# A fused two-block layer on one core: state outputs with the tables as moving operands, their regrouping on TensorE, and four smaller edits

## The chip, the core and the metric

The kernel runs on one core of a Trainium2 chip. The metric is the device time of one execution in microseconds (us); the median of three runs of the kernel before is 1020.39 us (1019.31 to 1023.4).

## The reference

Two blocks run one after the other on 512 tokens of width 1024, in fp32. The first is a norm, a gated causal convolution beside an attention over dilated windows, a projection of both (each normed first) that is added to x, and a gated feed-forward layer. The second block is the hybrid layer of which this change touches most:

```python
h = rms_norm_2(x, norm_g) * (1 + scale[:, None]) + shift[:, None]
xa, za, q, k, v, zb, qi, ki, wi, ga, gb = jnp.split(h @ w_in, IN_SPLITS, axis=-1)
ya = jax.nn.gelu(s5_mixer(xa, a_re, a_im, b_re, b_im, c_re, c_im, d_skip, log_dt))
g = ya @ w_glu + b_glu
ya = (g[..., :512] * jax.nn.sigmoid(g[..., 512:]) * jax.nn.silu(za)) @ w_a_o
yb = (dsa_mixer(q, k, v, qi, ki, wi) * jax.nn.silu(zb)) @ w_b_o
merged = jax.nn.sigmoid(ga) * ya + jax.nn.sigmoid(gb) * yb
x = x + gate[:, None] * (merged @ w_out)
return rms_norm_2(x, final_g)
```

`s5_mixer` is a state space model: 32 groups of 16 channels, each with 64 complex states, h_t = a h_(t-1) + B u_t and y_t = Re(C h_t) + D u_t. `dsa_mixer` is an attention that keeps the 128 best keys of each query.

## The kernel before

Activations lie as [features x 512 tokens]. A projection splits weights and activations into a high and a low part and issues three matmuls per 128 rows of the contraction (`mm3`, lines 193 to 195); in this text such a group is a triple. Weights stream through SP's queue in units of 512 KB, three units ahead, and are split by ACT (line 97) and DVE (line 98).

The order of TensorE's work is written as generators. The attention of a block asks for so many steps of a `filler` per head (`fill`), and each `yield` of a filler is a step; a tile scheduler then places the instructions of the other engines, with a priority lead (`high_priority`) for some.

*First block.* `mix_out` makes eight outputs of 128 rows, each of four triples (k = 0 to 3) over the normed branch, `ch`/`cl` for the convolution. The branch's root of the mean square (`rms`, then `rsqrt`: twelve DVE steps) is started at the first output; `spread` (line 236) turns it into a row on PE at the third. While the feed-forward layer runs, `ssm_tables` makes the tables of the state space model in four chunks, one `yield` at a time: `ca`, the table of the states' decays and C; `bts` (line 934); and `tt`, a block triangle of direct terms. They are stored to memory (`tabs`).

*Second block.* `gates` is the filler of the last attention: four projections for `szb`, four for `sza`, six of the eight for `thb` (tanh), then for each of the four chunks `chunk_out`, and after chunks 0 and 1 one more of the `thb`. `chunk_out(c)` copies the states into `hs` with GpSimd (POOL), loads `cat` and `tt` (two buffers under one tag, so the next chunk's loads wait for this chunk's matmuls), and issues for each of eight groups a matmul of `cat` with `hs` (line 1208) and one of `tt` with the inputs `U` (line 1209): table as the stationary operand of 128 x 128, 64 columns moving. Then comes gelu (ACT, DVE), eight stores `yad` and one load `yl` that bring the result from [step and channel x group and block] to [group and channel x time], and the split into `sh` and `sl` for the GLU projection.

The attention between those steps is scores (lines 254, 255), `z` (DVE, line 258), exp (ACT, line 262), transposes of the probabilities into two `tp` buffers of PSUM (line 306), their copies `pT` (ACT, line 312) and products with the values (line 283).

*Tail.* The final norm runs over two token halves: squares, a sum by PE (lines 1383, 1386), `rms_of` (DVE), `spread`, products and stores.

Of the kernel before, what the change touches and what calls it, by code (L numbers as in the profile page):

```python
# [9 lines left out]
F = mybir.dt.float32  # L10
R = mybir.dt.float32r
I32 = mybir.dt.int32
AF = mybir.ActivationFunctionType
OP = mybir.AluOpType
# [4 lines left out]
S = 512  # L19
D = 1024  # L20
P = 128
EPS = 1e-6
# [3 lines left out]
LEAD = 800  # L26
NT1 = 13
KS = 3
RAW = 3
WARM = 8  # L30
FILLA = (3.0, 4.0, 5.0, 2.6)
# [3 lines left out]
class K:  # L35
# [185 lines left out]

    def rms_of(self, pool, p, n, tag, room=None):
        toks = p.shape[1] // P
        d = pool.tile([P, 4, P], F, name="spd")[:, :toks]
        self.V.tensor_mul(d, p.rearrange("p (i t) -> p i t", t=P),
                          self.ident[:, None, :].to_broadcast([P, toks, P]))
        s = pool.tile([P, 4], F, name=tag + "s")[:, :toks]
        self.V.tensor_reduce(s, d, axis=AX.X, op=OP.add)
        return self.rsqrt(pool, s, 1.0 / n, EPS, tag, room)

# [85 lines left out]
    def mixer(self):  # L316
# [179 lines left out]
        def conv():  # L496
# [43 lines left out]
            for _ in range(3):  # L540
                yield
            yield from mix_out(ch, sqc)

        def mix_out(ys, sq):

            pend = []
            for n in range(8):
                if n % 2 == 0:
                    wh, wl = self.w()
                p = self.acc()  # L550
                cs = slice(n % 2 * P, n % 2 * P + P)
                yield from self.steps(p, (wh[:, :, cs], wl[:, :, cs]), ys)
                with self.tc.high_priority(offset=LEAD):
                    if n == 0:
                        r = self.rms(sm, [sq], 512, "rx")
                    if n == 2:
                        Rn = self.spread(sm, r, sm.tile([P, S], F, name="Rx"))
                pend.append((n, p))
                if n >= 2:
                    for m, p in pend:  # L560
                        t = at.tile([P, S], F, name="z", bufs=2)
                        V.tensor_mul(t, p, Rn)
                        V.tensor_add(x1[m], x1[m], t)
                    pend = []
                if n == 2:
                    for _ in range(4):
                        yield
# [10 lines left out]
        self.drain()  # L578
        self.run(mix_out(yh, sqa))
        cst.close()  # L580
# [4 lines left out]
    def ffn(self, x1):  # L585
# [10 lines left out]
        tabs = ExitStack()  # L596
        table = self.ssm_tables(tabs)
        for _ in range(2):
# [221 lines left out]

    def ssm_tables(self, st):
        nc, a, V, A, G, T = self.nc, self.a, self.V, self.A, self.G, self.T
# [51 lines left out]
        yield  # L874
        nr = p.tile([P, 48], F, name="snr")
        V.tensor_scalar(nr, pr[:, 1], -1.0, None, op0=OP.add)
# [27 lines left out]
        yield  # L904
        self.tabs = self.dram.tile([3, 4, P, S * 2], F, name="tabs")
        for c in range(4):
            gs = slice(8 * c, 8 * c + 8)
            def table(x, y, nj, name):
# [17 lines left out]
                                ca[:, :, 1:].rearrange("p g j x -> p g (j x)"))  # L926
            bts = p.tile([P, 8, P], F, name="bts", tag="io")
            kk = p.tile([16, 8, P], F, name="kk")
# [20 lines left out]
            V.tensor_add(kk[:, :, 0:16], kk[:, :, 0:16], de)  # L949
            tt = p.tile([P, 8, P], F, name="tt", tag="io")  # L950
            G.memset(tt, 0.0)
            for j in range(8):
                s = 7 - j
                nc.sync.dma_start(tt[16 * j:16 * j + 16, :, 16 * s:], kk[:, :, 0:P - 16 * s])
            nc.sync.dma_start(self.tabs[1, c], tt.rearrange("p g x -> p (g x)"))

# [57 lines left out]
    def hybrid(self, xs, second, close, out):  # L1014
# [174 lines left out]

        yad = self.dram.tile([4, P, S], F, name="yad")  # L1190
        y4 = yad.rearrange("j (g p) (s c) -> j s p g c", p=16, c=64)
        sv = []

        def chunk_out(sso, c):
# [10 lines left out]
            py = self.acc()  # L1205
            for g in range(8):
                o = py[:, g * 64:(g + 1) * 64]
                T.matmul(o, ca[:, g], hs[:, g], start=True, stop=False)  # L1208
                T.matmul(o, tt[:, g], U[:, 8 * c + g], start=False, stop=True)  # L1209
                yield  # L1210
            ys = sso.tile([P, S], F, name="ys")
# [5 lines left out]
            A.activation(y2, y2, AF.Tanh, scale=0.7978845608028654)  # L1217
            V.scalar_tensor_tensor(ys, y2, 1.0, ys, op0=OP.add, op1=OP.mult)
            for s in range(8):
                nc.sync.dma_start(y4[c, s], ys[16 * s:16 * s + 16].rearrange("p (g c) -> p g c", c=64))  # L1220
            yl = sso.tile([P, 8, 64], F, name="yl")
            nc.sync.dma_start(yl.rearrange("p s c -> p (s c)"), yad[c])
            sh = sso.tile([P, S], R, name=f"sh{c}")
            sl = sso.tile([P, S], R, name=f"sl{c}")
            v = yl.rearrange("p s c -> p c s")
            A.activation(sh.rearrange("p (c s) -> p c s", s=8), v, AF.Copy, scale=0.5)
# [5 lines left out]
        zb = []  # L1232

        sza = [zp.tile([P, S], F, name=f"sza{j}") for j in range(4)]
        thb = [zp.tile([P, S], F, name=f"thb{j}") for j in range(8)]

        def gates():
            for j in range(4):
                silu2(szb[j], (yield from self.proj(xs)))
                zb.append(szb[j])  # L1240
            for j in range(4):
                silu2(sza[j], (yield from self.proj(xs)))
            def tanhs(js):
                for j in js:
                    A.activation(thb[j], (yield from self.proj(xs)), AF.Tanh, scale=0.5)

            yield from tanhs(range(6))
            for _ in cin:
                pass
            s1.close()  # L1250
            sso = self.pool(ss, "ssmout", side="right")
            for c in range(4):
                yield from chunk_out(sso, c)
                yield from tanhs(range(6 + c, min(7 + c, 8)))

# [64 lines left out]
        for m in range(4):  # L1320
            pair(yb, thb[2 * m:2 * m + 2], m, lambda n: thb[n])
        glu()
        ss.close()
# [9 lines left out]
        for m in range(4):  # L1333
# [6 lines left out]
            for e in range(2):  # L1340
# [6 lines left out]
                mg.append((hi, lo))  # L1347
        sq = x3p.tile([P, S], F, name="sqE")
        ws = [self.w() for _ in range(2)]
        ps = [self.acc() for _ in range(2)]  # L1350
# [27 lines left out]
        def norm(e):  # L1378
# [6 lines left out]
            with self.tc.high_priority(offset=200):  # L1385
                T.matmul(p, self.ones, sqs[e][3], start=False, stop=True)
                r = self.rms_of(x3p, p, D, "re")
            for k in range(8):
# [15 lines left out]
        self.run(last(5, 1))  # L1404
        self.pad(x3p, 352)
        first, second = norm(0), norm(1)
# [39 lines left out]
def _layout(x):  # L1446
# [32 lines left out]
    o["win2v"] = _pack(np.concatenate([r(1600, 64), r(2752, 8)], axis=1), 8, 72)  # L1479
    w = f(x["w_glu_2"])[0]  # L1480
    o["wglu"] = _pack(w.reshape(512, 2, 4, P).transpose(0, 2, 1, 3).reshape(512, D), 4, 256)
# [35 lines left out]
```

## Time and profile before

| | us |
|---|---|
| median of three runs | 1020.39 |
| the profiled execution | 1019.43 |
| its span | 1017.6 |
| PE busy | 992.5 |
| DVE busy | 687.6 |
| ACT busy | 420.7 |
| POOL busy | 145.2 |

The span runs from the first to the last instruction that the profiler saw. Busy times are sums over an engine's instructions; PE's matmuls are pipelined and overlap in the records, so the distance between two starts tells what one costs, not its duration.

### The profile page before, as it was taken

The page shows a single profiled execution, that of the slowest core. Times are in us where ns is not written, and L with a number is a line of the kernel's source. Part 1 is how long each engine was busy: PE and PEld are TensorE (multiplying, and loading weights), DVE is VectorE, ACT ScalarE, POOL GpSimd, SP SyncE. Part 2 cuts the span into 40 slices and gives each one's busy share as a digit, 9 for nine tenths or more (in the row PEclk, how much of TensorE's full clock was granted, in tenths as well). Part 3 has the DMA queues.
Part 4 walks back from the last instruction along what each step waited for, and adds up shares of the span by engine and source line. Part 5 has one row for each costly group of instructions (what it writes and reads, how often), then busy time and mean ns, then how long its engine had stood idle before and what let it go on. Part 6 is the DMA issues. An engine that isn't in the chain of part 4 may idle for free.

```text
span 1017.6 us, 13862 instructions
## 1 busy us (share of the span) xinstructions
PE 992.5 (98%) x5074; PEld 824.4 (81%) x5074; DVE 687.6 (68%) x1334; ACT 420.7 (41%) x710; POOL 145.2 (14%) x324
## 2 busy tenths in 40 slices
PE   9999999999999999999999999999999979999995
PEld 7888887887777778888888898788888878888885
DVE  6886778786997847787653238599995555544444
ACT  6455556443333333233222225556445553333251
POOL 0000000007711100000010100001888130000020
PEclk9999999999999999999999999999999999999998
DMA  7343221223245576465552323343222352343212
GB/s 268 98 135 104 79 84 42 63 89 127 67 142 171 142 219 213 144 203 185 169 170 90 114 93 129 121 133 112 89 83 104 109 160 63 116 173 104 83 42 83
DMA packets 56100, 125.12 MB, mean 123 GB/s; under 512 B 17824, under 2 KB 24480, under 8 KB 55904
## 3 DMA queue, kind: packets, MB, share of 16 engines
q1 hardware_dynamic: 55888, 124.19, 37.6%
q8 instruction: 40, 0.66, 0.3%
q14 instruction: 28, 0.23, 0.1%
q10 hardware_dynamic: 144, 0.05, 0.0%
HBM read 110.45 MB, written 12.58 MB: 121 GB/s over the span
## 4 chain that ended last, share of the span: by engine, by line
PE 89%; DVE 3%; DMA 3%; POOL 3%; issue 1%; SPq 1%; ACT 0%; DVEq 0%; ACTq 0%; POOLq 0%
PE acc L193 24%; PE acc L195 23%; PE acc L194 23%; PE acc L376 2%; PE acc L374 2%; PE acc L375 2%; PE acc L283 2%; PE tp L306 2%; PE sc L255 1%; PE sc L254 1%; DVE wl L98 1%; POOL stt L751 1%; PE acc L1209 1%; PE acc L1152 1%; PE acc L1208 1%
## 5 line engine op out<-in xcount | busy, mean ns | idle before, releaser
L97 ACT CAST wh<-raw 128x1024 fp32r<-128x1024 f32 x156 | 161.6, 1037 | 300.0 <-PE acc L194 245.9
L98 DVE TENSOR_TENSOR wl<-raw,wh 128x1024 fp32r<-128x1024 f32 x156 | 188.8, 1211 | 92.8 <-ACT wh L97 91.3
L193 PE MATMUL acc<-fh,wh 128*128 128x512 f32 x336 | 133.1, 396 | 2.2 <-DVE gs L617 2.2
L195 PE MATMUL acc<-fh,wl 128*128 128x512 f32 x336 | 131.1, 390 | 0.0
L194 PE MATMUL acc<-fl,wh 128*128 128x512 f32 x336 | 131.0, 390 | 0.0
L193 PE MATMUL acc<-hh,wh 128*128 128x512 f32 (+1 forms) x280 | 111.7, 399 | 0.0
L195 PE MATMUL acc<-hh,wl 128*128 128x512 f32 (+1 forms) x280 | 109.6, 391 | 0.0
L194 PE MATMUL acc<-hl,wh 128*128 128x512 f32 (+1 forms) x280 | 109.4, 391 | 0.0
L193 PEld LDWEIGHTS acc<-fh,wh 128*128 128x128 f32 x336 | 63.1, 188 | 17.1 <-DVE gs L617 2.6
L195 PEld LDWEIGHTS acc<-fh,wl 128*128 128x128 f32 x336 | 63.1, 188 | 13.3
L193 PE MATMUL acc<-th,wh 128*128 128x512 f32 (+1 forms) x198 | 73.7, 372 | 0.0
L194 PEld LDWEIGHTS acc<-fl,wh 128*128 128x128 f32 x336 | 63.2, 188 | 12.9 <-issue 0.2
L195 PE MATMUL acc<-th,wl 128*128 128x512 f32 (+1 forms) x198 | 73.4, 371 | 0.0
L194 PE MATMUL acc<-tl,wh 128*128 128x512 f32 (+1 forms) x198 | 73.4, 371 | 0.0
L195 PEld LDWEIGHTS acc<-hh,wl 128*128 128x128 f32 (+1 forms) x280 | 52.2, 186 | 12.1
L262 ACT ACTIVATE e<-z,mn 128x128 f32<-128x128 f32 (+3 forms) x64 | 36.1, 564 | 61.0 <-DVE mn L258 60.8
L193 PEld LDWEIGHTS acc<-hh,wh 128*128 128x128 f32 (+1 forms) x280 | 52.3, 187 | 10.5 <-issue 1.2
L194 PEld LDWEIGHTS acc<-hl,wh 128*128 128x128 f32 (+1 forms) x280 | 52.3, 187 | 9.6
L1162 POOL TENSOR_TENSOR hm<-H,a 128x64 f32<-128x64 f32 x63 | 28.0, 444 | 116.0 <-ACT H L1156 111.1
L193 PEld LDWEIGHTS acc<-th,wh 128*128 128x128 f32 x198 | 37.3, 189 | 7.1
L194 PEld LDWEIGHTS acc<-tl,wh 128*128 128x128 f32 x198 | 37.3, 188 | 7.1
L195 PEld LDWEIGHTS acc<-th,wl 128*128 128x128 f32 x198 | 37.3, 188 | 7.0
(400 smaller groups left out, 2080.6 us busy)
## 6 DMA issues: line engine op xcount, KB each, us to landing
raw<-in_wgu SPq DMA_DIRECT2D x44, 512.0 KB, 3.6
raw<-in_win SPq DMA_DIRECT2D x37, 512.0 KB, 3.5
mraw<-in_wmod SPq DMA_DIRECT2D x24, 512.0 KB, 4.6
raw<-in_wout SPq DMA_DIRECT2D x16, 512.0 KB, 3.5
raw<-in_wdown SPq DMA_DIRECT2D x16, 512.0 KB, 3.5
raw<-in_wconv SPq DMA_DIRECT2D x12, 512.0 KB, 3.5
raw<-in_wqkv SPq DMA_DIRECT2D x10, 512.0 KB, 4.2
x<-in_xT SPq DMA_DIRECT2D x16, 256.0 KB, 5.0
```

The source lines that it names most:

```text
L97: self.A.copy(hi, raw)
L98: self.V.tensor_sub(lo, raw, hi.bitcast(F))
L193: self.T.matmul(out, lh, rh, start=start, stop=False)
L194: self.T.matmul(out, lh, rl, start=False, stop=False)
L195: self.T.matmul(out, ll, rh, start=False, stop=stop)
L262: self.A.activation(e[:, :n], z[:, :n], AF.Exp, bias=mn, scale=-1.0, accum_out=den)
L283: self.T.matmul(self.yp[64 * e:64 * e + 64, pr * P:(pr + 1) * P], value(j, 2 * pr + e), pTs[u - h0 + 2 * pr + e][:, j * P:(j + 1) * P], st ...
L306: self.T.transpose(pp[:, j * P:(j + 1) * P], e[:, j * P:(j + 1) * P], self.ident)
L374: T.matmul(ps[i], xh[k][:, t], wh[:, kk], start=k == 0, stop=False)
L375: T.matmul(ps[i], xh[k][:, t], wl[:, kk], start=False, stop=False)
L376: T.matmul(ps[i], xl[k][:, t], wh[:, kk], start=False, stop=k == 7)
L1162: G.tensor_mul(m, H[:, c - 1, None].to_broadcast([P, 2, 2, 16]), self.a8.rearrange("p (w r) g -> p w r g", w=2))
```

## The change

1. *State outputs.* In `chunk_out` the states (or `U`) become the stationary operand, 128 x 64, and the table the moving one, 128 columns; two groups go to the two partition halves of the output. The result then lies as [group parity and block x group, step, channel], and a new function `regroup` brings it to [.. channel x time] with sixteen 64x64 matmuls against the identity per chunk, into a `tp` buffer, from which `sh` and `sl` are read. The stores and loads `yad`, `yl` go. The rows of the GLU weights are permuted on the host to match.
2. *Gates.* Five of the `thb` come before chunk 0, then one after each of chunks 0 to 2, each followed by that chunk's `regroup`; `regroup(3)` runs after the first pair of output projections.
3. *Tables.* `tt` is no longer put together on chip: zeros and then the diagonals are stored straight to `tabs`. `bts` has a buffer of its own, a temporary of the tables is lent from the feed-forward layer's `gs`, and there is one more `yield` per chunk.
4. *Tail.* The root of the two final norms is 1/sqrt by ACT's square root, DVE's reciprocal and one Newton step; an early call of the square root is put ahead of the last projections.
5. *mix_out.* k = 0 to 2 of the first two outputs run before either k = 3; the root is started after the second (convolution) or the first (attention) of them. 6. Ten warm-up matmuls at the start instead of eight; a pad is smaller.

```diff
-WARM = 8
+WARM = 10
...
+    def root(self, pool, s, scale, eps):
+        sh = list(s.shape)
+        v, t, y = (pool.tile(sh, F, name="root" + c) for c in "vty")
+        V = self.V
+        V.tensor_scalar(v, s, scale, eps, op0=OP.mult, op1=OP.add)
+        self.A.activation(t, v, AF.Sqrt)
+        V.reciprocal(y, t)
+        V.scalar_tensor_tensor(v, v, -0.5, y, op0=OP.mult, op1=OP.mult)
+        V.tensor_mul(t, v, y)
+        V.scalar_tensor_tensor(y, t, 1.5, y, op0=OP.add, op1=OP.mult)
+        return y
...
-            yield from mix_out(ch, sqc)
+            yield from mix_out(ch, sqc, 1)
...
                 if n % 2 == 0:
                     wh, wl = self.w()
-                p = self.acc()
                 cs = slice(n % 2 * P, n % 2 * P + P)
-                yield from self.steps(p, (wh[:, :, cs], wl[:, :, cs]), ys)
+                if n == 0:
+                    p, p1 = self.acc(), self.acc()
+                    c1 = slice(P, 2 * P)
+                    for e, (q, c) in enumerate(((p, cs), (p1, c1))):
+                        yield from self.steps(q, (wh[:, :, c], wl[:, :, c]), ys, range(3))
+                        if e == late:
+                            with self.tc.high_priority(offset=LEAD):
+                                r = self.rms(sm, [sq], 512, "rx")
+                    yield from self.steps(p, (wh[:, :, cs], wl[:, :, cs]), ys, range(3, 4))
+                elif n == 1:
+                    p = p1
+                    yield from self.steps(p, (wh[:, :, cs], wl[:, :, cs]), ys, range(3, 4))
+                else:
+                    p = self.acc()
+                    yield from self.steps(p, (wh[:, :, cs], wl[:, :, cs]), ys)
                 with self.tc.high_priority(offset=LEAD):
-                    if n == 0:
-                        r = self.rms(sm, [sq], 512, "rx")
                     if n == 2:
...
+            yield
+            tt = self.tabs[1, c].rearrange("p (g x) -> p g x", g=8)
+            nc.sync.dma_start(tt[0:112, :, 0:112], zt[0:112, None].to_broadcast([112, 8, 112]))
-            bts = p.tile([P, 8, P], F, name="bts", tag="io")
+            bts = p.tile([P, 8, P], F, name="bts")
...
-            tt = p.tile([P, 8, P], F, name="tt", tag="io")
-            G.memset(tt, 0.0)
             for j in range(8):
                 s = 7 - j
                 nc.sync.dma_start(tt[16 * j:16 * j + 16, :, 16 * s:], kk[:, :, 0:P - 16 * s])
-            nc.sync.dma_start(self.tabs[1, c], tt.rearrange("p g x -> p (g x)"))
...
-            for g in range(8):
-                o = py[:, g * 64:(g + 1) * 64]
-                T.matmul(o, ca[:, g], hs[:, g], start=True, stop=False)
-                T.matmul(o, tt[:, g], U[:, 8 * c + g], start=False, stop=True)
-                yield
+            pys = py.rearrange("q (s g p) -> q s g p", s=8, p=16)
+            for g in range(0, 8, 2):
+                for n in range(2):
+                    for e in range(2):
+                        T.matmul(pys[64 * e:64 * e + 64, :, g // 2],
+                                 U[:, 8 * c + g + e] if n else hs[:, g + e],
+                                 tt[:, g + e] if n else ca[:, g + e], start=n == 0, stop=n == 1)
+                    yield
...
-            V.scalar_tensor_tensor(ys, y2, 1.0, ys, op0=OP.add, op1=OP.mult)
+            yts[c] = yt = sso.tile([P, S], F, name="yt")
+            V.scalar_tensor_tensor(yt, y2, 1.0, ys, op0=OP.add, op1=OP.mult)
+
+        def regroup(sso, c):
+            pt = self.tp()
             for s in range(8):
-                nc.sync.dma_start(y4[c, s], ys[16 * s:16 * s + 16].rearrange("p (g c) -> p g c", c=64))
-            yl = sso.tile([P, 8, 64], F, name="yl")
-            nc.sync.dma_start(yl.rearrange("p s c -> p (s c)"), yad[c])
+                for e in range(2):
+                    r = slice(64 * e, 64 * e + 64)
+                    T.matmul(pt[r, 64 * s:64 * s + 64], yts[c][r, 64 * s:64 * s + 64], self.ident[r, r],
+                             start=True, stop=True)
             sh = sso.tile([P, S], R, name=f"sh{c}")
             sl = sso.tile([P, S], R, name=f"sl{c}")
-            v = yl.rearrange("p s c -> p c s")
+            v = pt.rearrange("p (s c) -> p c s", c=64)
...
-            yield from tanhs(range(6))
+            yield from tanhs(range(5))
...
+            rest.append(lambda: regroup(sso, 3))
             for c in range(4):
                 yield from chunk_out(sso, c)
-                yield from tanhs(range(6 + c, min(7 + c, 8)))
+                if c < 3:
+                    yield from tanhs(range(5 + c, 6 + c))
+                    regroup(sso, c)
...
             pair(yb, thb[2 * m:2 * m + 2], m, lambda n: thb[n])
+            if m == 0:
+                rest.pop()()
...
+        one = x3p.tile([P, 1], F, name="one")
+        A.activation(one, self.ones[:, 0:1], AF.Sqrt)
...
-                r = self.rms_of(x3p, p, D, "re")
+                r = self.rms_of(x3p, p, D, "re", root=True)
```

Three places show how the order of the instructions moves (each row: line, operation, output tile and inputs, shape, count; the changed kernel's lines are 13 to 45 higher).

**PE between chunks 0 and 1.** Before, the projection's last triple and a pair of scores, then chunk 1 (`cat`, `hs`, `U`, `tt` are the operands of the state outputs, `tp` the transposes' PSUM buffer):

```order
L193 MATMUL acc<-hh_4634,wh 128x512
L194 MATMUL acc<-hl_4635,wh 128x512
L195 MATMUL acc<-hh_4634,wl 128x512
L254 MATMUL sc<-kh,q_6299 128x512
L255 MATMUL sc<-kl,q_6299 128x512
L1208 MATMUL acc<-hs,cat 128x64
L1209 MATMUL acc<-U,tt 128x64
L306 MATMUL tp<-ident,e 128x128 x6
```

Now:

```order
L193 MATMUL acc<-hh_4630,wh 128x512
L194 MATMUL acc<-hl_4631,wh 128x512
L195 MATMUL acc<-hh_4630,wl 128x512
L269 MATMUL sc<-kh,q_6359 128x512
L270 MATMUL sc<-kl,q_6359 128x512
L1258 MATMUL tp<-ident,yt 64x64 x16
L1237 MATMUL acc<-cat,hs 64x8x16 x2
L321 MATMUL tp<-ident,e 128x128 x8
L298 MATMUL acc<-pT,vt 64x128 x12
L1237 MATMUL acc<-tt,U 64x8x16 x2
```

The regroup (line 1258) stands ahead of chunk 1 and of the eight transposes, which need both `tp` buffers, one after the other. On ACT, in the same stretch, the changed kernel has the read of the regroup's buffer ahead of the copies of the probabilities:

```order
L277 ACTIVATE e,den<-z,mn 128x512
L1263 ACTIVATE sh_7940<-tp 128x512
L327 COPY pT<-tp 128x512 x2
L277 ACTIVATE e,den<-z,mn 128x512
L1242 COPY ys<-acc 128x512
```

Before, the read into `sh` was of `yl` and stood behind the copies.

**DVE at the end of the root of the convolution branch** (`rxy` is what the spread on PE waits for, `z` belongs to a score of the attention). Before:

```order
L209 TENSOR_TENSOR rxt<-rxv,rxy 128x4
L210 SCALAR_TENSOR_TENSOR rxy<-rxt,rxy 128x4
L491 TENSOR_REDUCE sqy<-s2y 128x128
L258 ISA z,mn<-sc,lc 128x512
L258 ISA mn 128x1
```

Now:

```order
L210 SCALAR_TENSOR_TENSOR rxy<-rxt,rxy 128x4
L212 SCALAR_TENSOR_TENSOR rxv<-rxt,rxv 128x4
L273 ISA z,mn<-sc,lc 128x512
L273 ISA mn 128x1
L209 TENSOR_TENSOR rxt<-rxv,rxy 128x4
L210 SCALAR_TENSOR_TENSOR rxy<-rxt,rxy 128x4
```

The last two steps of the root moved behind a `z`; it is the one of the score that stands just before the spread on PE.

**ACT at the early call of the square root** (`one`) and at the first real one, in the changed kernel; before, the only table load of the program is its first:

```order
L97 CAST wh<-raw 128x1024
L1393 ACT_TABLE_LOAD
L1393 ACTIVATE one<-ones 128x1
L1356 ACTIVATE yah_8656<-th 128x512
L97 CAST wh<-raw 128x1024
L1380 ACT_TABLE_LOAD
L1380 ACTIVATE th<-acc 128x512
...
L1434 ACTIVATE x_8665<-x_8665,cols 128x256
L228 ACT_TABLE_LOAD
L228 ACTIVATE roott<-rootv 128x2
```

The early call was placed ahead of the last tanh (line 1380), so the table is changed back for that and again for the root.

## Rows read from the trace of the kernel before

**Rows 1.** The page: busy time by engine; shares of the chain that ended last.

```profile
PE 992.5 (98%) x5074; PEld 824.4 (81%) x5074; DVE 687.6 (68%) x1334; ACT 420.7 (41%) x710; POOL 145.2 (14%) x324
...
PE 89%; DVE 3%; DMA 3%; POOL 3%; issue 1%; SPq 1%; ACT 0%; DVEq 0%; ACTq 0%; POOLq 0%
```

**Rows 2.** PE's waits: line <- releaser: us in total, times, longest.

```profile
PE acc L1208 <- DMA cat<-tabs: 5.5, 1, 5.5
PE tp L236 <- DVE rey L210: 4.0, 3, 3.2
PE acc L193 <- DVE gs L617: 2.2, 1, 2.2
PE tp L933 <- ACT bts L934: 1.7, 1, 1.7
...
PE acc L194 <- DVE cl L504: 0.8, 1, 0.8
...
PE tp L940 <- DVE ca L920: 0.5, 1, 0.5
```

**Rows 3.** Windows: us, busy by engine (instructions), granted clock PEclk, DMA share, GB/s.

```profile
250.00:270.00 20.00, 17.28 (x79) 13.86 (x79) 17.27 (x55) 6.26 (x9) 17.63 (x42) 1.00 0.17 54
830.00:850.00 20.00, 14.07 (x110) 13.09 (x109) 9.06 (x16) 9.01 (x15) 4.02 (x6) 0.83 0.41 120
```

**Rows 4.** Timeline at chunk 3: start, us, engine, line, tiles [idle before <- releaser].

```profile
833.71 0.32 SPq L1202 DMA_DIRECT2D cat<-tabs  x1
...
833.98 3.89 POOL L1199 COPY hs<-H 64x252 f32<-64x252 f32 x4
...
839.38 0.66 PE L1208 MATMUL acc<-hs,cat 128*128 128x64 f32 x2 [5.47 <-DMA cat<-tabs]
...
840.50 0.69 PE L1209 MATMUL acc<-U,tt 128*128 128x64 f32 x2 [0.46 <-DMA tt<-tabs]
...
841.12 3.50 PE L283 MATMUL acc<-pT,vt 128*64 128x128 f32 x32
```

**Rows 5.** Timeline of PE: state outputs of chunk 2, line 283, triples of a projection.

```profile
822.61 1.97 PE L283 MATMUL acc<-pT,vt 128*64 128x128 f32 x32
...
824.51 0.50 PE L193 MATMUL acc<-hh,wh 128*128 128x512 f32 x1
...
825.31 0.40 PE L193 MATMUL acc<-hh,wh 128*128 128x512 f32 x1
...
826.00 0.39 PE L193 MATMUL acc<-hh,wh 128*128 128x512 f32 x1
...
831.06 0.39 PE L1208 MATMUL acc<-hs,cat 128*128 128x64 f32 x2
...
831.51 0.39 PE L1208 MATMUL acc<-hs,cat 128*128 128x64 f32 x2
```

**Rows 6.** Timeline after chunk 1: its gelu chain, and ACT's reads of PSUM and `yl`.

```profile
819.01 1.10 ACT L1226 ACTIVATE sh<-yl 128x512 fp32r<-128x512 f32 x1 [0.62 <-DMA yl<-yad]
...
820.40 0.48 PE L254 MATMUL sc<-kh,q 128*128 128x512 f32 x1
...
823.34 1.05 ACT L312 COPY pT<-tp 128x512 f32<-128x512 f32 x2
...
825.68 3.63 SPq L1220 DMA_DIRECT2D yad<-ys  x8
```

**Rows 7.** Timeline at the spread of the first mix_out.

```profile
179.38 1.05 PE L236 MATMUL tp<-ident,rxy 128*128 128x128 f32 x8
...
179.73 0.68 DVE L258 CUSTOM_DVE_ANT_0 z<-sc,lc 128x512 f32<-128x512 f32 x1
```

**Rows 8.** Timeline of ACT at the start, and of DVE in the tail's second root.

```profile
1.17 1.28 ACT L64 ACT_TABLE_LOAD   x1 [1.17 <-PEq L1507]
...
1008.52 0.17 DVE L204 TENSOR_SCALAR rev<-res 128x2 f32<-128x2 f32 x1
...
1010.45 0.16 DVE L210 SCALAR_TENSOR_TENSOR rey<-ret,rey 128x2 f32<-128x2 f32 x1
```

More of the change, by code (lines that the diff above doesn't have):

```diff
@@ L220, in rms, with rms_of @@
         return self.rms_of(pool, p, n, tag, room)
-    def rms_of(self, pool, p, n, tag, room=None):
+    def root(self, pool, s, scale, eps):
[9 more added lines that the diff above has]
+        return y
+    def rms_of(self, pool, p, n, tag, room=None, root=False):
         toks = p.shape[1] // P
@@ L228, in rms_of @@
         self.V.tensor_reduce(s, d, axis=AX.X, op=OP.add)
+        if root:
+            return self.root(pool, s, 1.0 / n, EPS)
         return self.rsqrt(pool, s, 1.0 / n, EPS, tag, room)
@@ L541, in conv, with mix_out @@
                 yield
-            yield from mix_out(ch, sqc)
-        def mix_out(ys, sq):
+            yield from mix_out(ch, sqc, 1)
+        def mix_out(ys, sq, late):
             pend = []
@@ L578, in mixer @@
         self.drain()
-        self.run(mix_out(yh, sqa))
+        self.run(mix_out(yh, sqa, 0))
         cst.close()
@@ L596, in ffn @@
         tabs = ExitStack()
-        table = self.ssm_tables(tabs)
+        table = self.ssm_tables(tabs, lambda: wg.tile([P, S], F, name="gs", bufs=2)[:, :48])
         for _ in range(2):
@@ L819, in sincos, with ssm_tables @@
         return out
-    def ssm_tables(self, st):
+    def ssm_tables(self, st, room):
         nc, a, V, A, G, T = self.nc, self.a, self.V, self.A, self.G, self.T
@@ L874, in ssm_tables @@
         yield
-        nr = p.tile([P, 48], F, name="snr")
+        nr = room()
         V.tensor_scalar(nr, pr[:, 1], -1.0, None, op0=OP.add)
@@ L905, in ssm_tables @@
         self.tabs = self.dram.tile([3, 4, P, S * 2], F, name="tabs")
+        zt = p.tile([P, 112], F, name="zt")
+        G.memset(zt, 0.0)
         for c in range(4):
@@ L1188, in hybrid @@
             q.extend(stack(p, 2 * c, 0.125, ap, "q"))
-        yad = self.dram.tile([4, P, S], F, name="yad")
-        y4 = yad.rearrange("j (g p) (s c) -> j s p g c", p=16, c=64)
-        sv = []
+        sv, yts = [], {}
         def chunk_out(sso, c):
@@ L1232, in hybrid @@
         zb = []
+        rest = []
         sza = [zp.tile([P, S], F, name=f"sza{j}") for j in range(4)]
@@ L1404, in hybrid @@
         self.run(last(5, 1))
-        self.pad(x3p, 352)
+        self.pad(x3p, 320)
         first, second = norm(0), norm(1)
@@ L1479, in _layout @@
     o["win2v"] = _pack(np.concatenate([r(1600, 64), r(2752, 8)], axis=1), 8, 72)
-    w = f(x["w_glu_2"])[0]
+    w = f(x["w_glu_2"])[0].reshape(4, 4, 2, 16, D).transpose(0, 2, 1, 3, 4).reshape(512, D)
     o["wglu"] = _pack(w.reshape(512, 2, 4, P).transpose(0, 2, 1, 3).reshape(512, D), 4, 256)
```

## The prediction

> **What bounds the kernel now.** I read the page's busy shares and chain first. TensorE (PE) is busy 98% of the 1017.6 us span and carries 89% of the chain that ended last [rows 1], so an edit counts only where it changes PE's own work or one of PE's waits; work on the other engines and the DMA queues is cover. The table of PE's waits comes next [rows 2]: the largest piece is one wait of 5.5 us in the state outputs (line 1208, for the table load `cat<-tabs`), then 4.0 us for the tail's root (three waits, the longest 3.2). The windows show what the large one does to the clock: 0.83 in 830 to 850 us, with PE busy only 14.07 of 20 us, while it stayed at 1.00 in 250 to 270, where PE's wait of 2.2 us for `gs` lies [rows 2, 3]. The timeline of that place shows why [rows 4]: chunk 3 follows chunk 2 at once, its buffers come free only when chunk 2's last matmul has read them, so the load is issued at 833.71 and POOL's copies of the states start at 833.98 while PE already waits; the matmuls begin at 839.38, and the 32 matmul records of line 283 behind them take 3.50 us, where the same group took 1.97 before [rows 4, 5].
>
> The profiled execution took 1019.43 us, 1.8 of it around the span. I make the sum against it; the median of the runs, 1020.39, stands 0.96 above, which I add at the end.
>
> **The state outputs, chunk 3.** The change puts one projection (eight triples of matmuls at 826.00 - 825.31 = 0.69 us [rows 5], 5.5 us), eight transposes and the regroup matmuls between chunk 2 and chunk 3, over 8 us in all, where nothing stood. POOL's copies need 3.89 us [rows 4] and the `cat` load 839.38 - 833.71 = 5.7, so both fit, with some 2 us of room; for `tt` PE waited 0.46 more, which fits too. This takes away 5.5 + 0.5 us of waiting [rows 2, 4] and the slow clock behind it: 3.50 - 1.97 = 1.5 us on line 283 and about 0.4 on each of the two pairs that ran before it (0.62 us from 840.50 to 841.12, where such a pair takes 0.22) [rows 4, 5]. Sum: **-8.3**.
>
> **The same matmuls, operands exchanged.** Before, two groups' four records start 0.45 us after the last two (831.06, 831.51) and a chunk has eight such steps: 3.6 us. The new form has 64 stationary and 128 moving columns, with outputs alternating between two partition halves. That is line 283's form exactly: 32 records in 824.51 - 822.61 = 1.90 us, 0.06 each [rows 5]. A chunk has 32 such records, so 1.9. New are the 16 regroup matmuls of a chunk, fp32, 64x64. No row shows them. Two records each, at line 283's 0.06 (the nearest row in stationary columns), make 1.9; half of that if the two array corners work side by side, 3.5 at line 1208's 0.11. I take 1.9. So 1.9 + 1.9 - 3.6 = +0.2 a chunk, +1.0 for four with the roundings. PE now changes its tile form about four times more in a chunk; the first matmul of a triple after such a change lasts 0.50 us, in a steady triple 0.40 (824.51 and 825.31 [rows 5]), so between 0 and 0.1 each, I take 0.07: **+1.0 + 1.1 = +2.1**.
>
> The 36 small DMAs through memory (`yad`, `yl`) leave SP's queue; nothing on the path waited for them alone, so 0. The regroup waits for the gelu chain, which took 825.68 - 820.40 = 5.3 us from the first matmul after a chunk's last to the use of its result [rows 6]; PE has about 7.5, 7.5, 6.4 and 5.5 us of other work there in the new order (8 to 11 triples, with scores and transposes), so 0, though the last cover is bare.
>
> **A new wait behind the regroup.** After regroups 0 and 1 PE comes to eight transposes of probabilities into two PSUM buffers. The regroup holds one of the two until ACT and VectorE (DVE) have read it, so the second four need the first four copied out; on ACT the copy `sh` (1.10 us) now stands ahead of that copy (two take 1.05) [rows 6]. From the regroup's end ACT needs 0.2 + 1.1 + 0.5, PE reaches the place after 0.2 + 0.4: about 1.15 us of waiting, twice: **+2.3** (0 if ACT is earlier, +4 if the other two regroups catch it as well).
>
> **mix_out.** Running k = 0 to 2 of two outputs first hides the 0.8 us wait for `cl` [rows 2]. But the square sum is issued later, and DVE's last two root steps now stand behind the `z` step of the score that PE issues just before the spread. In the trace the spread starts at 179.38, that `z` at 179.73 and lasts 0.68 [rows 7]; with its short read-out and two steps of 0.2 [rows 8] the root is ready near 180.9. So 1.5 appears where 0.8 goes: **+0.7** (-0.8 if the scheduler's order costs nothing, +0.7 at most).
>
> **State tables.** `bts` gets its own buffer and the zeroed table goes by memory, so the wait of `L933` for ACT's `bts`, itself behind the `tabs<-tt` store, goes, and one more yield per chunk gives `ca` time: -1.7 - 0.5 [rows 2] = **-2.2** (0 if something else is late there: DVE is busy 17.27 of 20 us in that stage [rows 3]). The 2.2 us for `gs` stays, the change does not touch it. Four more DMAs of zeros on SP go in between two weight loads that are three units ahead of their use: 0. The last table ends 13 triples or 9 us later, still before PE needs it: 0.
>
> **Tail.** Twelve DVE steps 0.2 us apart (1008.52 to 1010.45 and its 0.16) [rows 8] become one step, ACT's square root and four steps. With two hand-overs that is some 1.3 us for 2.1: -0.8, all bare. In the first of the two norms the wait of 0.4 goes if the table load is done by then. The early call that is to bring the root's table in is placed by the scheduler ahead of the last tanh calls, so ACT loads three times: two loads in the merge stage, where ACT has idle time, and one right before the first root. One load took 1.28 us [rows 8]; ACT has nothing else to do there until the argument comes, so most of it is hidden; bare, it takes the first norm's gain and 0.9 more. Together **-1.2** (-1.2 to +0.1). The Trainium skill (ScalarE: Activation LUTs, section What ACT_TABLE_LOAD costs) adds a drain of about 1.38 us to each load. By that the first norm would wait about 1.4 us longer and the sum be 1.4 higher; the row of this kernel, at its start, shows the load alone. Two more warm-up matmuls lie in the first wait for data: 0 (to +0.3).
>
> **Sum.** -8.3 + 2.1 + 2.3 + 0.7 - 2.2 - 1.2 = -6.6: 1012.8 on the profiled execution, **1013.8** as a median. About 0.5%, 5.1 us, is what a measurement of this kernel can tell from no change: faster means under 1015.3, slower over 1025.5.
>
> **Rivals.**
> - *Corners side by side.* The regroup's two halves use opposite corners of the array; if they overlap, a record costs 0.03 and a chunk saves 0.95, of which `sh` (which starts no earlier than the `e` step ahead of it) gives some back after chunks 0 and 1: -2.4, so 1011.4. Against it: line 283, whose two outputs lie side by side in two column halves, starts no record sooner than 0.06 us after the last [rows 5]. For it: no group of this trace uses two row halves. The Trainium skill (TensorE: Matmul & The Clock Gate, section Part 3: Packing small matmuls - row/col tiling) says such matmuls run concurrently and a weight load overlaps only across row groups; no run shows it yet. Chance 0.22.
> - *The regroup as dear as full-size loads.* 0.11 a record, +1.6 a chunk: 1020.3, no change. Against it: line 283 at 64 columns. 0.09.
> - *The change does not do what it says at chunk 3:* loads slower than their cover, PE waits as before, and the clock falls: 1013.8 + 8.3 = 1022. Against it: over 8 us of cover for 5.7. 0.07.
> - *Slower: the clock falls at the regroups.* The chain of copies and tanh in front of each regroup slips behind other DVE and ACT work, PE idles there beyond the 2.2 us after which the clock stayed up, toward the 5.5 after which it did not [rows 2, 3]; at 3.5 us a regroup costs 3.5 of waiting (two of them 1.15 less, already counted) and 2.3 of slow clock: 4 x 5.8 - 2.3 = 21, so 1035. One or two such regroups leave it at 1018 to 1025, it decides from three on. Against it: cover of 5.5 to 7.5 us for a chain of 5.3. 0.05.
> - *Moved waits:* the tables' removed 2.2 us come back elsewhere in that full stage and the table load lies bare: 1017.5. 0.07.
>
> My own case has 0.50, mostly 1011.5 to 1016, some 15% of it above 1015.3. **Chances:** faster 0.22 + 0.85 x 0.50 = 0.65 (rounded); slower 0.05; the rest, 0.30, no change. **Range:** 1008.5 (side by side, no wait behind the regroup at chunks 0 and 1, mix_out at its best end) to 1020.5 (the dear regroup); outside are the bare chunk 3, the slower case and little below.
>
> **What would show it.** PE's waits without `cat<-tabs`; the clock at 1.00 through the whole state-output stage; the output matmuls at 1.9 us a chunk; 16 regroup matmuls in 1.9 us; a wait of about 1.15 us of the transposes for ACT's copies after the first two regroups; one of about 1.5 at the spread near 180 us; `L933` without a wait; twelve steps fewer in the tail, with three more table loads on ACT. I am wrong if the regroup shows a wait over 3 us, if chunk 3 still waits for its tables, or if the gap near 180 us is missing.

## The result, and the profile after

| | before | after |
|---|---|---|
| median of the runs, us | 1020.27 | 1011.69 |
| lowest and highest | 1019.31, 1023.4 | 1010.75, 1012.76 |
| the profiled execution | 1019.43 | 1010.75 |
| its span | 1017.6 | 1009.0 |

The ratio of the medians is 0.9906, with a 95% interval of 0.9882 to 0.9930: 8.6 us faster. The forecast was 1013.8, with a range of 1008.5 to 1020.5.

First PE's busy time and the chain of the changed kernel, from the page (against [rows 1]):

```profile
PE 991.3 (98%) x5206; PEld 819.7 (81%) x5206; DVE 683.2 (68%) x1320; ACT 424.5 (42%) x716; POOL 139.9 (14%) x321
...
PE 92%; POOL 3%; DVE 2%; ACT 1%; issue 1%; DMA 1%; DVEq 0%; SPq 0%; POOLq 0%
```

PE still sets the time. Its busy time fell by only 1.2 us; most of the rest was waiting. The table of PE's waits (against [rows 2]):

```profile
PE tp L251 <- DVE rooty L232: 2.3, 1, 2.3
PE acc L193 <- DVE gs L643: 2.2, 1, 2.2
PE tp L251 <- DVE rxy L210: 1.4, 1, 1.4
PE tp L321 <- ACT pT L327: 1.4, 2, 0.7
...
PE tp L321 <- DVE e L280: 1.0, 1, 1.0
```

The 5.5 us for `cat<-tabs`, the 1.7 of `L933`, the 0.8 for `cl` and the 0.5 for `ca` are gone. Three are new: 1.4 at the spread for `rxy`, 1.4 at the transposes for ACT's `pT` (twice 0.7), and 1.0 at other transposes for `e`. The windows of the two stages where the clock matters (the columns of [rows 3]; the kernel before has a clock of 1.00 in the first of these two stretches and of 0.86 in the second):

```profile
255.00:270.00 15.00, 12.79 (x50) 10.04 (x49) 12.54 (x35) 4.62 (x8) 13.11 (x31) 0.89 0.19 68
825.00:850.00 25.00, 25.00 (x253) 21.16 (x250) 13.06 (x23) 10.53 (x17) 3.37 (x6) 1.00 0.27 95
```

The state outputs keep the full clock. But it fell elsewhere, at 255 to 270 us, behind the old wait for `gs`. It also fell at the last spread of the tail: the clock is 0.62 in 1000 to 1003 us. I come back to both.

The starts of the same matmuls in the two profiled executions split the 8.7 us between their spans (1017.65 and 1008.98 before rounding):

| from, to | before | after | difference |
|---|---|---|---|
| start to the first matmul of mix_out | 163.23 | 163.15 | -0.1 |
| to the first of the feed-forward layer | 60.98 | 62.54 | +1.6 |
| to the first of the second block's projections | 385.78 | 384.39 | -1.4 |
| to the first score of the last attention | 96.71 | 96.72 | 0.0 |
| to the first of the GLU (the state outputs) | 162.89 | 155.43 | -7.5 |
| to the first of the last projections | 87.47 | 87.47 | 0.0 |
| to the end | 60.59 | 59.28 | -1.3 |

### The profile page after: what moved, and what is told of

The parts are those of the page before. It is cut to its first block, busy times and chain, and to the rows that moved or that the text cites. A ratio compares the mean times of both kernels' runs of the same rounds, so it can differ in the third digit from the quotient of the medians.

```text
span 1009.0 us, 14032 instructions
## 1 busy us (share of the span) xinstructions
PE 991.3 (98%) x5206; PEld 819.7 (81%) x5206; DVE 683.2 (68%) x1320; ACT 424.5 (42%) x716; POOL 139.9 (14%) x321
## 4 chain that ended last, share of the span: by engine, by line
PE 92%; POOL 3%; DVE 2%; ACT 1%; issue 1%; DMA 1%; DVEq 0%; SPq 0%; POOLq 0%
PE acc L193 25%; PE acc L194 24%; PE acc L195 24%; PE acc L391 2%; PE acc L389 2%; PE acc L390 2%; PE acc L298 2%; PE tp L321 2%; PE sc L270 1%; PE sc L269 1%; POOL stt L777 1%; PE acc L1237 1%; PE acc L1181 1%; PE tp L251 1%; PE acc L1055 1%
```

## The experiments

**The order alone.** The kernel before with five of the tanh projections ahead of the chunks and one behind each of the first three; nothing else.

```diff
-            yield from tanhs(range(6))
+            yield from tanhs(range(5))
...
-                yield from tanhs(range(6 + c, min(7 + c, 8)))
+                if c < 3:
+                    yield from tanhs(range(5 + c, 6 + c))
```

> The kernel before with one edit: five tanh projections ahead of chunk 0 and one after each of chunks 0 to 2 (the old matmul form, the stores and loads through memory and all else stay). If the wait at chunk 3 and the slow clock behind it come from chunk 3 following chunk 2 at once: PE's wait for cat<-tabs goes (5.5 to under 0.5 us), the clock is 1.00 through the stage, and the time falls by 7.5 to 8.5 us, to about 1012. Rival, the loads and copies are slow of themselves and the new matmul form is what gives the gain: a wait of 2 us or more for cat or hs stays at chunk 3, and the time falls by less than 5 us.

Measured: 1011.77, ratio 0.9921 (0.9891 to 0.9951). No wait for `cat` or `hs`, and the window of the stage:

```profile
825.00:850.00 25.00, 25.00 (x165) 21.87 (x165) 13.57 (x23) 11.34 (x17) 3.69 (x6) 1.00 0.37 119
```

The stage from the first score to the GLU took 154.52 us, 8.4 less than before and 0.9 less than in the changed kernel. That edit alone accounts for the stage; the new matmul form with its regroup adds 0.9 on top. The median too is level with that of the whole change (1011.69): in the table above, the 2.7 us that the tables and the tail gained stand against the 2.5 lost in `mix_out` and the new form.

**The old order, all else new.**

```diff
-            yield from tanhs(range(5))
+            yield from tanhs(range(6))
...
-                if c < 3:
-                    yield from tanhs(range(5 + c, 6 + c))
-                    regroup(sso, c)
+                yield from tanhs(range(6 + c, min(7 + c, 8)))
+                if c < 2:
+                    regroup(sso, c)
+                if c == 3:
+                    regroup(sso, 2)
```

> The changed kernel with the old order of the gates (six tanh projections first, chunk 3 straight behind chunk 2; the regroup of chunk 2 moved behind chunk 3 so that it waits for nothing). If the order carries the gain: a wait of 5 to 6 us for cat or hs at chunk 3 comes back, the clock falls to half behind it for some microseconds, and the time is 6.5 to 8.5 us above the changed kernel's 1011, so 1017 to 1020. Rival, the new form needs no such cover (its matmuls and the transposition through memory were what was late): less than 3 us above.

Measured: 1016.91 in one run, just under the expected 1017 to 1020; the stage took 162.56 us, 7.1 more than in the changed kernel. The timeline at chunk 3 (start, duration, then as in [rows 4]):

```profile
833.68 0.32 SPq L1229 DMA_DIRECT2D cat<-tabs  x1
...
837.51 0.69 PE L1237 MATMUL acc<-cat,hs 128*64 128x128 f32 x4 [3.65 <-DMA cat<-tabs]
...
837.96 3.65 PE L298 MATMUL acc<-pT,vt 128*64 128x128 f32 x32
```

The wait and the slow clock are back (clock 0.86 in 825 to 850). The wait is 3.65 us and not the 5 to 6 I expected. The load took 3.8 us where it took 5.7 [rows 4]. The stores of `yad` did not run beside it before: they were issued at 838.82, 0.6 us before PE went on. Ahead of it in SP's queue stood a unit of weights, issued behind the load of `yl` at 831.70 in the kernel before, and at 830.95 here, where there is no `yl`. Whether that is why the load took longer was not tried.

**The regroup corner after corner.**

```diff
-            for s in range(8):
-                for e in range(2):
+            for e in range(2):
+                for s in range(8):
                     r = slice(64 * e, 64 * e + 64)
```

> The changed kernel with the sixteen regroup matmuls of a chunk in another order: eight in one corner of the array, then eight in the other, instead of alternating. If the 1.08 us per chunk (0.034 a record) come from the two corners working side by side: about 0.06 a record, 1.8 to 1.9 us per chunk, and 2 to 3 us more in all. Rival, a 64x64 matmul is that cheap by its size: 1.1 us per chunk as before and no change in time.

The first regroup and what follows it, in the changed kernel:

```profile
805.74 1.15 PE L1258 MATMUL tp<-ident,yt 64*64 64x64 f32 x32
...
806.82 0.44 PE L1237 MATMUL acc<-cat,hs 128*64 128x128 f32 x4
```

and with one corner after the other:

```profile
805.05 1.90 PE L1258 MATMUL tp<-ident,yt 64*64 64x64 f32 x32
...
806.88 0.44 PE L1237 MATMUL acc<-cat,hs 128*64 128x128 f32 x4
```

From the start of the regroup to the start of what follows it is 1.08 us against 1.83, that is 0.034 a record against 0.057 (a record is one entry of the trace; each of these matmuls leaves two); the stage is 3.0 us longer (158.45), the time 1013.4 in one run. The price at which I had put the regroup, 0.06, is that of one corner; the alternating order halves it.

**mix_out as before.** The body of `mix_out` and its two calls are those of the kernel before:

```diff
-                if n == 0:
-                    p, p1 = self.acc(), self.acc()
...
+                p = self.acc()
+                yield from self.steps(p, (wh[:, :, cs], wl[:, :, cs]), ys)
                 with self.tc.high_priority(offset=LEAD):
+                    if n == 0:
+                        r = self.rms(sm, [sq], 512, "rx")
```

> The changed kernel with mix_out as it was before (the first output whole, then the second). By my reading of the two traces mix_out lost 1.5 us on this stretch (a wait of 0.96 at the transposes near 168 us and of 1.43 at the spread near 180 us for one of 0.77): both waits go, one of 0.8 for cl comes back, and the time is 1.4 to 1.6 us below the changed kernel's. Rival, the waits only move and the stretch stays as long: within 0.3 us on the stretch from the first mix_out matmul to the spread.

Measured: 1008.87, ratio to before 0.9889 (0.9855 to 0.9923), an interval that overlaps the changed kernel's. From the first mix_out matmul to the spread it took 16.17 us, against 17.64 in the changed kernel: -1.5, as expected; both waits are gone and the 0.8 for `cl` is back. The timeline of the changed kernel at the end of that stretch (against [rows 7]) shows the mechanism that was forecast:

```profile
179.68 0.68 DVE L273 CUSTOM_DVE_ANT_0 z<-sc,lc 128x512 f32<-128x512 f32 x1
...
180.48 0.16 DVE L210 SCALAR_TENSOR_TENSOR rxy<-rxt,rxy 128x4 f32<-128x4 f32 x1
...
180.79 1.13 PE L251 MATMUL tp<-ident,rxy 128*128 128x128 f32 x8 [1.43 <-DVE rxy L210]
```

And the place where the removed 0.8 us came back, 12 us ahead of that: PE no longer waits for `cl`, so it reaches the transposes sooner than DVE has the probabilities.

```profile
167.84 0.67 DVE L273 CUSTOM_DVE_ANT_0 z<-sc,lc 128x512 f32<-128x512 f32 x1
...
168.51 0.86 DVE L280 TENSOR_SCALAR e<-e,rd 128x512 f32<-128x512 f32 x2
...
169.12 0.63 PE L321 MATMUL tp<-ident,e 128*128 128x128 f32 x4 [0.96 <-DVE e L280]
```

In these profiles most of the 1.5 us is not kept. At the spread of the feed-forward layer's norm PE waits 1.2 to 1.6 us in the three profiles with the old `mix_out` and the new tables, and 0 to 0.9 in the six of the changed kernel's code up to there. DVE waits there for a chain of POOL operations, of which the same one lasts 0.3 us in one run and 1.3 in another. Whether the old order brings that wait is open: with the old tables beside it, in the kernel before and in the order alone, it is 0.5 and 0. From the first mix_out matmul to the second block, less 1.6 us in the profiles in which the clock fell near 264 us, those three took 445.1 to 445.5 us and the six 445.2 to 446.2: about 0.4 less on average. The median lies 2.8 us under the changed kernel's; these stretches do not explain that much.

**The root started earlier.**

```diff
-            yield from mix_out(ch, sqc, 1)
+            yield from mix_out(ch, sqc, 0)
```

> The changed kernel with the root of the convolution branch started after the first of the two interleaved outputs instead of the second. If the wait of 1.43 us at the spread near 180 us comes from DVE's last root steps standing behind the z step of the score: the root now ends before that z, the wait goes, and the stretch from the first mix_out matmul to the spread is 0.9 to 1.5 us shorter (up to 0.5 may come back as a wait for the square sum). Rival, the start of the chain is what counts and the steps stay late: the wait stays above 1 us.

A miss (1010.42 in one run). The wait at the spread went, and that for `e` too, but PE now waits for the square sum:

```profile
167.54 0.68 DVE L528 TENSOR_TENSOR sqc<-sqc,s2c 128x512 f32<-128x512 f32 x1
...
168.28 1.13 PE L219 MATMUL tp<-sqc,ones 128*128 128x512 f32 x2 [2.00 <-DVE sqc L528]
```

The stretch to the spread is 17.14 us, 0.5 less than in the changed kernel and 1.0 more than with the old mix_out. DVE is what is late in this stretch; each order of PE's work meets it at another place.

**The regroup in another PSUM buffer.**

```diff
-            pt = self.tp()
+            pt = self.acc()
```

> The changed kernel with the regroup's output in one of the four acc buffers of PSUM instead of one of the two tp buffers. If the wait behind regroups 0 and 1 is for the tp buffer that the regroup holds until sh and sl have been read: both waits of the transposes for ACT's pT (0.68 us each) go, the two groups of eight transposes take 0.8 to 0.9 us instead of 1.92, and the stage from the first score to the GLU is 1.4 to 2.1 us shorter. Rival, ACT is what is late there (sh stands ahead of the copies of the probabilities, whatever buffer it reads) or an acc buffer is now missed elsewhere: a wait of the same size stays, change under 0.5 us.

In the changed kernel, behind the first regroup:

```profile
807.19 0.66 PE L321 MATMUL tp<-ident,e 128*128 128x128 f32 x4
...
807.36 0.57 ACT L1263 ACTIVATE sh<-tp 128x512 fp32r<-128x512 f32 x1
...
807.88 0.59 ACT L327 COPY pT<-tp 128x512 f32<-128x512 f32 x1
...
808.52 0.65 PE L321 MATMUL tp<-ident,e 128*128 128x128 f32 x4 [0.68 <-ACT pT L327]
```

with the `acc` buffer:

```profile
808.83 1.09 PE L321 MATMUL tp<-ident,e 128*128 128x128 f32 x8
809.00 0.58 ACT L1263 ACTIVATE sh<-acc 128x512 fp32r<-128x512 f32 x1
...
809.52 1.07 ACT L327 COPY pT<-tp 128x512 f32<-128x512 f32 x2
```

The eight transposes run through, both waits are gone, and the stage is 1.8 us shorter (153.67), though ACT still has `sh` ahead of `pT`. So it was the buffer. (1010.89 in one run; its profile is 1.6 us behind the changed kernel's by 340 us, before the edit.)

**The tail as before**, with no early square root:

```diff
-        one = x3p.tile([P, 1], F, name="one")
-        A.activation(one, self.ones[:, 0:1], AF.Sqrt)
...
-                r = self.rms_of(x3p, p, D, "re", root=True)
+                r = self.rms_of(x3p, p, D, "re")
```

> The changed kernel with the twelve-step root on DVE in the tail, no square root and no early call. If the tail's gain is the shorter chain: from the last projection matmuls on the kernel is 1.1 to 1.3 us longer, the wait at the last spread 3.2 instead of 2.3, and the wait of 0.4 at the first spread is back; the stage with the two extra table loads (near 885 us) is as long as with them. Rival, the loads cost something on the path there: that stage becomes shorter by 0.3 us or more.

Measured: 1012.57 in one run. From the first of the last projections to the start of the last spread it is 1.62 us longer (53.75 against 52.13), more than the 1.1 to 1.3 expected; to the end of the span it is 1.1, because in the changed kernel's profile the clock fell at that spread and in this one it did not. The wait at the last spread is 3.18, that at the first 0.48. The stages around the two extra table loads are equal within 0.02 us. The changed kernel's ACT at the first root and PE at the last spread (against [rows 8]):

```profile
990.50 1.28 ACT L228 ACT_TABLE_LOAD   x1
991.79 0.20 ACT L228 ACTIVATE roott<-rootv 128x2 f32<-128x2 f32 x1
...
1001.82 1.20 PE L251 MATMUL tp<-ident,rooty 128*128 128x128 f32 x4 [2.29 <-DVE rooty L232]
```

The last spread with the old root; its four matmuls take 0.68 us at the full clock, where the changed kernel's took 1.20:

```profile
1004.14 0.68 PE L251 MATMUL tp<-ident,rey 128*128 128x128 f32 x4 [3.18 <-DVE rey L210]
```

**The old matmul form, old mix_out, the rest new.** `chunk_out` as before, with its stores and loads; no `regroup`; the GLU weights unpermuted.

```diff
-            for g in range(0, 8, 2):
...
+            for g in range(8):
+                o = py[:, g * 64:(g + 1) * 64]
+                T.matmul(o, ca[:, g], hs[:, g], start=True, stop=False)
+                T.matmul(o, tt[:, g], U[:, 8 * c + g], start=False, stop=True)
+                yield
```

> The changed kernel with the state outputs in the old form (tables stationary, result through memory) and mix_out as before; the order of the gates, the tables and the tail stay changed. By the traces the new form with its regroup saved 1.5 us of matmul time against the old one at full clock, but with its waits and form changes was 0.9 us longer than the old form in the new order. If so: the stage from the first score to the GLU is 0.7 to 1.1 us shorter than in the changed kernel, and the time about 1007.5 to 1008.5. Rival, the new form pays: the stage is 1 us or more longer.

Measured: 1008.4, ratio to before 0.9866 (0.9836 to 0.9896). The stage took 154.52 us, 0.9 less than in the changed kernel and equal to that of the order alone. In this stage the new form pays only with its buffer freed: 153.67.

**What was found, together:** old mix_out, `acc` for the regroup, no early square root.

> The changed kernel with mix_out as before, the regroup's output in an acc buffer, and no early square root. If the effects found apart add up: 1.5 us less up to the feed-forward layer, 1.8 us less from the first score to the GLU, the tail within 0.1 us of the changed kernel's, so 3.2 us below the changed kernel: 1007 to 1008.5 as a median, below the kernel before by more than 1%. Rival, the early call is needed: the tail is 0.5 us or more longer, with a wait at the first spread.

Measured: 1008.61, just above the expected span, ratio to before 0.9865 (0.9846 to 0.9885), under both kernels. PE does not wait at the first spread, so the early call is not needed: with it or without it ACT loads the table again just ahead of the first root. But the tail was not as expected. The last spread starts 0.3 us later after the first of the last projections than in the changed kernel (52.44 against 52.13), and the span ends 0.6 later than in the changed kernel's second profile (59.42 against 58.78), both with the full clock at that spread. The matmuls of those projections start 0.233 us apart at 512 columns and 0.117 at 256, where they start 0.227 and 0.120 apart in all eleven other profiles. The tile `one` of the early call lies in the same pool as a pad that the change had made smaller, and the pad was not set anew here; that the tiles' places in memory are the cause was not tried.

The median is 3.1 us under the changed kernel's, with intervals of the ratio that just touch. The two profiles do not show 3.1: this one is 1.5 below the changed kernel's first and 0.2 above its second. The runs lie at 1007.5 to 1007.9, with a granted clock of 0.996 and 0.997, and at 1009.4 to 1009.9, with 0.994 and 0.995; the next run shows what one such difference is. The kernel is not told apart from the two variants at 1008.4 and 1008.9.

**The changed kernel again.** No edit.

> The changed kernel itself, a second profile. Its first profile has eight matmuls at half clock near 264 us, some 3 us behind the wait of 2.2 us for gs, which cost 1.6 us; the kernel before and several variants with the same wait show none. If the fall depends on when in the run that wait comes and not on the code: this profile may show the stretch at full clock, and the feed-forward stage is then 1.4 to 1.6 us shorter at the same waits. Rival, the code decides (what stands around the wait): the same eight matmuls at half clock again.

Its window (against the one above, 0.89):

```profile
255.00:270.00 15.00, 12.79 (x59) 10.32 (x59) 12.54 (x38) 5.74 (x9) 13.10 (x31) 1.00 0.22 72
```

The same wait of 2.2 us, the clock up, and the feed-forward layer 1.6 us shorter; 1009.42 in one run. So the code alone does not decide whether the clock falls at that place. (In the first profile the slow matmuls begin at 263.59, 0.9 us behind the end of the wait and not 3.)

## Why the prediction was right, and where its steps were not

*Chunk 3, -8.3.* Right: -8.4 by the order alone, and 7.1 comes back with the old order. Cover was the whole matter: in the changed kernel the load of `cat` was issued at 827.54 and PE came to it at 835.28, 7.7 us later.

*The exchange and regroup, +2.1.* The step that failed is the price of the regroup: "Two records each, at line 283's 0.06". They took 0.034 and the regroup 1.08 us a chunk in place of 1.9. This was my first rival, at 0.22, and its time, 1011.4, is nearer the result than my own. I had no row with two row halves in use, and set against it a row in which they were not; that row could not speak on it. The Trainium skill (TensorE: Matmul & The Clock Gate, section Part 3: Packing small matmuls — row/col tiling) says that matmuls in different tiles of the array run at the same time, and that a weight load overlaps with matmuls in flight only where the row group differs. The trace agrees: 0.034 alternating, 0.057 not. The other term held: the output matmuls took 8.2 us in all for 128 records, form changes included (0.064 each). The matmuls of this step came to -1.6 us against the old ones at full clock (8.2 + 4.3 against 14.1 in the run of the order alone), and scores and triples after a change of form to about +1. With the wait behind the regroup removed, the stage was 0.8 us shorter than with the order alone: -0.8 where the forecast had +2.1.

*The wait behind the regroup, +2.3.* Right in place and cause, too large in size: PE waited 2 x 0.68, and the `acc` buffer gave back 1.8. I took `sh` at the 1.10 us that it took from `yl`; from PSUM it takes 0.57.

*mix_out, +0.7.* Right in mechanism, 0.8 too small: it cost 1.6 up to the feed-forward layer. The wait for `cl` was booked as removed; it came back 2 us on, at the transposes (169.12; the wait for `cl` was at 166.98). I had asked what is late next only at the spread.

*Tables, -2.2.* Both waits went. The layer was 1.4 us shorter in the profile, where the clock cost 1.6, and 3.0 in the second profile, where the wait of 0.5 at the norm's spread, behind the POOL chain, was gone as well. The forecast said nothing of the clock there; that the wait for `gs` stays was right.

*Tail, -1.2.* Right in mechanism, too small in size; the -1.3 of the profile is nearer by luck. The last spread starts 1.56 us earlier after the first of the last projections (52.13 against 53.69), and undone this cost 1.62. In the profile 0.5 us went to the clock at that spread; in the second profile, where the clock stayed up, the tail is 1.8 shorter than before. The load ahead of the first root was hidden, as taken: it ended 0.3 us after the root's argument was ready, and the root was ready 1.0 us before PE came to the spread. Of the drain that the Trainium skill (ScalarE: Activation LUTs, section What ACT_TABLE_LOAD costs) adds to a load no row here shows anything: the square root started 0.01 us after the load's end.

The sum, -6.6, missed 2.1 of the 8.7 between the profiles, and it is nearer than its terms because they cancel in part: the exchange with its regroup was put 2.9 too dear (the regroup alone 3.3) and the wait behind it 0.5, the gains of tables and tail 1.4 too small at the full clock; mix_out was put 0.8 too cheap, and the clock, which the sum did not have, cost 2.1. That the time lies inside the range is so in part luck. The rivals on chunk 3 and on the clock at the regroups fell: PE did not wait for its tables or at a regroup. So did that of a regroup as dear as full-size loads.

## What to carry to other kernels

A gain of several parts may be that of one: here a change of order gave the whole of the stage, and the rewritten matmuls lost 0.9 us until their output left a buffer that other work needed. When a wait is removed, follow the engine that was late to the next place where PE meets it, and not only to the place the change names; the 1.5 us that the old mix_out gave back on its own stretch had shrunk to about 0.4 by the end of the next layer. And a price taken from a row holds for the form of that row only: where the new operation uses another part of the array or reads another memory, keep both ends open.

## What the hardware showed beyond that

- fp32 matmuls of 64x64 in opposite corners of the array, issued in turn, start 0.034 us a record apart; issued corner by corner 0.057.
- The clock fell to half behind the same wait of 2.2 us in five of the ten profiles of the changed kernel and its variants, of the changed kernel itself in one of two, and in neither of the two profiles with the old code there. Each time about eight matmuls of 512 columns ran at 0.427 us instead of 0.228:

```profile
262.74 0.50 PE L193 MATMUL acc<-fh,wh 128*128 128x512 f32 x1 [2.21 <-DVE gs L643]
...
263.59 0.63 PE L193 MATMUL acc<-fh,wh 128*128 128x512 f32 x1
264.01 0.63 PE L194 MATMUL acc<-fl,wh 128*128 128x512 f32 x1
```

  That is 1.6 us, as much as several edits here. I had taken 2.2 us as a wait after which the clock stays up, from one profile.
- At the last spread, behind a wait of 2.3 us (3.2 with the old root), the matmuls started 0.21 us apart in eight of all twelve profiles, at half clock, and 0.11 in the other four. So a tail compared between two profiles can differ by 0.5 us with the same code; compare it up to the start of that spread.
- ACT read the same 128x512 values, reordered in the same way, in 0.57 to 0.60 us from PSUM and in 1.08 to 1.13 from SBUF (four reads each).
